# Sums of the down weights' blocks, formed in memory by adding transfers: issued one or three at a time behind named steps, with the block as the outer dimension of the scratch array

## The chip, the cores and the metric

The kernel runs on one core of a Trainium2 chip. The metric is the device time of one execution in microseconds (us), the median of several runs, lower is better. The core has TensorE (PE, matrix products), VectorE (DVE), ScalarE (ACT), GpSimd (POOL) and the SyncE queue (SP). SP, ACT and POOL issue transfers (DMAs); all of them are carried by the same 16 DMA engines. An adding transfer, whose destination becomes the sum of what it held and what arrives, is issued from POOL here.

## The reference, cut to what matters

One decoder block over 512 tokens of width 1024, all in float32:

```python
h = rms_norm(x, norm_mix_pre)
xr, gr, q, k, v, iq, ik, iw, g_a, g_b = split(h @ w_in)
y_a = (rg_lru(causal_depthwise_conv(xr)) * gelu(gr)) @ w_rnn_out
y_b = dsa_sparse_attention(rope(q), rope(k), v, iq, ik, iw) @ w_att_out   # top 128 keys of 512
merged = sigmoid(g_a) * y_a + sigmoid(g_b) * y_b
x = x + rms_norm(merged @ w_o, norm_mix_post)
h = rms_norm(x, norm_ffn_pre)
f = (silu(h @ w_ffn_gate) * (h @ w_ffn_up)) @ w_ffn_down                  # 1024 -> 2816 -> 1024
out = x + rms_norm(f, norm_ffn_post)
```

The last product, by w_ffn_down, is done with the seven-product block scheme of Strassen and Winograd. It needs sums of four 128 x 512 blocks of the weight for each of 11 pairs of row tiles; these sums are what the change is about.

## The kernel before

**Precision.** Each float32 operand is split into a high part and a low remainder (type fp32r), and a product is three matmuls: high by high, high by low, low by high (`mm3`, lines 285, 287 and 289). For most tiles of w_in the low part is made by the DMA engines: POOL loads the tile as the high part (`do_load`, line 221, 512 KB), ACT writes its negative (`do_split`, line 247), and POOL adds the tile onto that with an adding transfer (line 248). These units pass through four "ws" and four "raw" slots and are loaded a few units ahead.

**Stages.** After the input norm come the indexer, the gate and recurrence projections (lines 632 to 643), one gate, one key and two query projections (706), then eight output projections of the recurrent branch (`rnn_out(0)` to `rnn_out(7)`, line 709; weights come through SP, line 231, and DVE forms the gated result `ma[m]` at line 653). Then attention: 16 heads by 4 query tiles are 64 units (line 793). Each unit has its logits, exponentials, transposes of the probabilities (line 752) and, at the end of a head, the product with the values (762). A pair of heads ends with a split of its output into `ot` by ACT and DVE (778). Between the steps of the units, 14 remaining projections are fed in a fixed share (`fill`, line 781): six of the queries, one key tile and seven gates; queries and keys need the rotary embedding (`rope`, line 475: a shuffle on DVE, line 479, two multiplications on POOL, lines 480 and 481, and a sum on DVE, 482). Here TensorE's order is pinned to the order in the program (`state["ordered"]`). After attention come eight output projections (line 816), each with a product on DVE (819), a sum on POOL (820) and a split; then w_o, the norms and the feed-forward part.

**The sums.** For each of 11 pairs j, `u_dram[j]` (1 MB of device memory) is filled in four steps by `down_sums` (line 686): SP lays down four blocks with one transfer (692); an adding transfer of 512 KB adds a block to the first two (694); one of 256 KB adds the first to the third (696); one of 256 KB adds the third to the fourth (also 696). Each step of a pair needs the step before it. Pairs go in groups of three (GROUP = 3; the last has two), and a call of `down_sums(n)` issues step 0 of group n, step 1 of group n-1, step 2 of group n-2 and step 3 of group n-3 together: 3 to 9 transfers. There are seven calls: behind rnn_out(1) and rnn_out(5) (line 712), and in heads 2, 5, 8, 11 and 14 (line 799). In the feed-forward part `load_d` (line 1073) loads each `u_dram[j]` into two tiles of 512 KB.

**Order.** The order on each engine comes from a planner that simulates the program; every engine then runs its instructions strictly in that order. `tc.issue_after(ins)` puts what follows behind `ins` on the engine of `ins`, and does not wait for its end. A transfer that POOL issues waits on POOL until its data and its room are ready, and all that is behind it on POOL waits too.

Of the kernel before, what the change touches and what calls it, by code (L numbers as in the profile page):

```python
# [9 lines left out]
F32 = mybir.dt.float32  # L10
F32R = mybir.dt.float32r
AF = mybir.ActivationFunctionType
A = mybir.AluOpType
AX = mybir.AxisListType

P = 128
S = 512
D = 1024
KT = D // P
NT = S // P  # L20
D_FF = 2816
FT = D_FF // P
# [23 lines left out]
def hybrid_block(ctx: ExitStack, tc: tile.TileContext, x, norm_mix_pre, w_in, conv_w, conv_b, rg_w_a,  # L46
# [4 lines left out]
    V, SC, G, PE = nc.vector, nc.scalar, nc.gpsimd, nc.tensor  # L51
    ld = nc.sync.dma_start
# [5 lines left out]
    small = ctx.enter_context(tc.tile_pool(name="small", bufs=4))  # L58
# [2 lines left out]
    ps_scope = ExitStack()  # L61
    ps_mix = ps_scope.enter_context(tc.tile_pool(name="ps_mix", bufs=1, space=bass.MemoryType.PSUM))

    GROUP = 3
    dram = ctx.enter_context(tc.tile_pool(name="dram", bufs=1, space=bass.MemoryType.DRAM))

    def acc():
        return psum.tile([P, 512], F32, name="acc", tag="acc")
# [4 lines left out]
    def ps_t():  # L73
        return ps_mix.tile([P, 512], F32, name="ps_t", tag="t", bufs=2)

    def ps_o():
        return ps_mix.tile([P, 512], F32, name="ps_o", tag="o", bufs=1)

    def f(ap):
        return ap.bitcast(F32)  # L80

    after = {}

    def split(src, hi, lo, lo_engine=None):
        return SC.copy(hi, src).ins, (lo_engine or V).tensor_tensor(lo, src, f(hi), op=A.subtract).ins  # L85
# [33 lines left out]
    def heap(shape, dt=F32R, name="hp"):  # L119
        return mixp.tile(shape, dt, name=name, tag="heap", bufs=14)  # L120
# [76 lines left out]
    state = {"load": 0, "split": 0, "ordered": False}  # L197
# [64 lines left out]
    def take(u, ahead=3):  # L262
        load_ahead(u)
        while state["split"] <= min(u + ahead, state["load"] - 1):
            s = state["split"]
            if units[s][3] == "r" or s > u + 2 and units[s][3] == "s":
                break
            do_split(s)
            state["split"] += 1
        return wss.pop(u)  # L270
# [7 lines left out]
    def pe(ins):  # L278
        if state["ordered"]:
            tc.keep_in_program_order(ins)  # L280
# [11 lines left out]
    def mm3(*args, **kw):  # L292
        for _ in mm3_steps(*args, **kw):
            pass
# [77 lines left out]
    for k0 in (0, 4):  # L372
        ks = slice(k0, k0 + 4)
        for cs in (slice(0, 256), slice(256, TOKW)):
            with tc.issue_after(after["hn"]), tc.issue_after(after["sqrt"]):
                ins = split(w_tok[:, ks, cs], tokw[:, 0, ks, cs], tokw[:, 1, ks, cs], G if k0 == 0 else V)
# [69 lines left out]
    sp = mixp.tile([P, KT], F32, name="sp")  # L446
# [24 lines left out]
    ma = [map_.tile([P, S], F32, name=f"ma{m}") for m in range(KT)]  # L471
# [73 lines left out]
    def drain(n):  # L545
        for _ in range(min(n, len(background))):
            background.pop(0)()
# [101 lines left out]
    def rnn_out(m):  # L649
        ps = acc()  # L650
        mm3(ps, take(u_ya[m]), lambda k: ys[k][:, 0, :], lambda k: ys[k][:, 1, :])
        SC.activation(ma[m], ma[m], AF.Sigmoid)
        V.tensor_tensor(ma[m], ps, ma[m], op=A.mult)
# [27 lines left out]


    NJ = FT // 2
    u_dram = [dram.tile([P, 4, 512], F32, name=f"u_dram{j}") for j in range(NJ)]

    def down_sums(n):
        for step, g in enumerate(range(n, n - 4, -1)):
            for j in range(GROUP * g, min(GROUP * g + GROUP, NJ)) if g >= 0 else ():
                u = u_dram[j]
                with tc.issue_after(after["pool"]), tc.issue_after(after["sp"]):  # L690
                    if step == 0:
                        ld(u, t_dn[j])
                    elif step == 1:
                        G.dma_start(u[:, 0:2], t_dn2[j], accum_op=A.add)
                    else:
                        G.dma_start(u[:, step:step + 1], u[:, 2 * step - 4:2 * step - 3], accum_op=A.add)

    def gate_b(m):
        ps = acc()
# [9 lines left out]
    for m in range(KT):  # L709
        rnn_out(m)  # L710
        drain(4)
        if m in (1, 5):
            down_sums(m // 4)
    drain(len(background))

    pts = []
# [29 lines left out]
    def probs(u):  # L746
        h, i = divmod(u, NT)
        pt, sm = pts[h % 2], sms.pop(u)
        w = (i + 1) * P
        pp = ps_t()  # L750
        for j in range(i + 1):
            pe(PE.transpose(pp[:, j * P:(j + 1) * P], sm[:, j * P:(j + 1) * P], ident))  # L752
        src = pp[:, 0:w].rearrange("p (j c) -> p j c", c=P)
        split(src, pt[:, 0, i:4 * i + 1:3, :], pt[:, 1, i:4 * i + 1:3, :])

    def values(h):
        pt = pts[h % 2]
        ps = ps_o()
        spans = [(0, 0, 4), (1, 4, 3), (2, 8, 2), (3, 11, 2)]
        for n, (j, b, w) in enumerate(spans):  # L760
            for part in range(2):
                pe(PE.matmul(ps[:, S - w * P:S], vst[j // 2][:, j % 2, h // 4, :], pt[:, part, b:b + w, :],
                             start=(n == 0 and part == 0), stop=(n == 3 and part == 1)))
        if h % 2 == 1:
            rb, pr = state["rb"], ps_t()
            for i in range(NT):
                pe(PE.transpose(pr[:, i * P:(i + 1) * P], rb[:, i], ident))
        ob = attp.tile([HD, S], F32, name="ob", tag="ob", bufs=1)
        SC.copy(ob, ps[HD:P])
        if h % 2 == 0:  # L770
            state["o"] = attp.tile([P, S], F32, name="o", tag="o", bufs=2)
        o = state["o"]
        off = (h % 2) * HD
        V.tensor_tensor(o[off:off + HD], ps[0:HD], ob, op=A.add)
        if h % 2 == 1:
            V.tensor_tensor(o, pr, o, op=A.mult)
            ot = heap([P, 2, S], name="ot")
            split(o, ot[:, 0, :], ot[:, 1, :])
            os_.append(ot)

    def filler():
        for kind, m in fill:
            yield from {"q": queries, "k": keys, "g": gate_b}[kind](m)
# [9 lines left out]
    for u in range(n_units):  # L793
        if u + AHEAD < n_units:
            logits(u + AHEAD)
        probs(u)
        if u % NT == LAG and u >= NT:
            values(u // NT - 1)
            if u // NT % 3 == 2:
                down_sums(2 + u // NT // 3)  # L800
        while done < START + (u + 1) * (n_fill - START) // n_units:
            next(fills, None)
            done += 1
# [5 lines left out]
    gb = []  # L809
    for m in range(KT):  # L810
        t = tmpp.tile([P, S], F32, name="gb", tag="t0")
# [4 lines left out]
    for m in range(KT):  # L816
        ps = acc()
        mm3(ps, take(u_yb[m]), lambda k: os_[k][:, 0, :], lambda k: os_[k][:, 1, :])
        V.tensor_tensor(gb[m], ps, gb[m], op=A.mult)
        G.tensor_tensor(gb[m], gb[m], ma[m], op=A.add)  # L820
        t = heap([P, 2, S], name="mg")
        split(gb[m], t[:, 0, :], t[:, 1, :])
        mg.append(t)
# [67 lines left out]
    for t in range(NT):  # L891
# [16 lines left out]
        r = neg2_rstd(ss[:, 0:1], 1, ss[:, 1:2])  # L908
# [161 lines left out]
    w_dn = w_ffn_down.rearrange("(j e p) c -> e p j c", e=2, p=P)  # L1070
    raw_d, ws_d, as_d = {}, {}, {}

    def load_d(j):
        raw_d[j] = []
        for c in range(2):
            t = raw_tile(c, [P, 2, 512])
            ld(t, u_dram[j][:, 2 * c:2 * c + 2, :])
            raw_d[j].append(t)

    def prep_d(j):  # L1080
# [23 lines left out]
    NJ = FT // 2  # L1104
# [178 lines left out]
```

## Time and profile before

| | us |
|---|---|
| median of three runs (907.73 to 910.62) | 908.67 |
| the profiled execution | 908.55 |
| its span, first to last instruction | 906.8 |
| TensorE busy in it | 850.8 |
| DVE busy | 678.1 |
| ACT busy | 524.1 |
| POOL busy | 259.5 |

A profiled execution records each instruction with its engine, start and duration, and for idle time of an engine the instruction or transfer that ended it (the releaser). TensorE is busy for most of the span, so the places to look at are those where it is not. The granted clock of TensorE is shown per stretch as a share: 1.00 is its higher level (2.4 GHz), 0.5 its lower one (1.2 GHz). The share of the DMA engines counts the time of packets, which can overlap, so it can be above 1. "Landing" is the time from a transfer's issue to the arrival of its last data.

### The profile page before, as it was taken

What the parts mean: (1) busy time and instruction counts of PE and PEld (TensorE: products, weight loads), DVE (VectorE), ACT (ScalarE), POOL (GpSimd) and SP (SyncE); (2) the same over time, 40 slices, a digit from 0 to 9 for tenths busy, and PEclk for the clock granted to TensorE, in tenths of its full rate; (3) what the DMA queues carried; (4) which work ended last, traced back from release to release, by engine and by line L of the source; (5) the groups of instructions that cost most, each with busy time, mean ns of one, the idle gap of its engine ahead of it and who ended that gap; (6) DMA issues with size and microseconds to landing.
All of it is one profiled execution on the core that took longest, in us unless ns stands there. A gap on an engine that the chain in (4) does not pass through costs nothing.

```text
span 906.8 us, 13184 instructions
## 1 busy us (share of the span) xinstructions
PE 850.8 (94%) x4745; PEld 735.5 (81%) x4745; DVE 678.1 (75%) x1235; ACT 524.1 (58%) x902; POOL 259.5 (29%) x276
## 2 busy tenths in 40 slices
PE   8999999999897989498999998899999999999996
PEld 5787888877686778487878887799999999988885
DVE  6686989976851487357756647988888788799996
ACT  5355457978321778376754435666566656566581
POOL 3262234552502444253002200233333333110000
PEclk9999999999899899799999999999999999999999
DMA  8488888759599797998354563667787878847623
GB/s 291 102 173 186 163 161 175 162 125 259 163 319 195 164 168 195 176 209 165 116 161 152 186 199 116 162 162 172 189 180 178 181 181 189 215 161 236 203 93 139
DMA packets 75316, 161.46 MB, mean 178 GB/s; under 512 B 9858, under 2 KB 33474, under 8 KB 75075
## 3 DMA queue, kind: packets, MB, share of 16 engines
q0 software_dynamic: 23184, 73.41, 42.3%
q1 hardware_dynamic: 50912, 85.11, 29.2%
q10 hardware_dynamic: 1154, 2.10, 0.6%
q8 instruction: 37, 0.61, 0.3%
q14 instruction: 29, 0.23, 0.1%
HBM read 154.31 MB, written 29.36 MB: 203 GB/s over the span
## 4 chain that ended last, share of the span: by engine, by line
PE 53%; DVE 14%; DMA 12%; issue 9%; ACT 6%; POOL 4%; SPq 1%; DVEq 0%; ACTq 0%; POOLq 0%
PE acc L285 6%; PE acc L287 6%; PE acc L289 6%; DMA ws<-in_t_ff_dram 5%; PE bank L1012 5%; PE bank L1010 4%; PE bank L1011 4%; PE bank L1102 2%; PE bank L1100 2%; PE bank L1101 2%; DVE xc L585 2%; PE acc L1010 2%; PE acc L1011 1%; PE acc L1012 1%; DMA ws<-in_t_in_dram 1%
## 5 line engine op out<-in xcount | busy, mean ns | idle before, releaser
L289 PE MATMUL acc<-hT,ws 128*128 128x512 f32 x248 | 99.8, 403 | 7.2 <-DMA ws<-in_t_in_dram 7.2
L85 DVE TENSOR_TENSOR ws<-raw,ws 128x1024 fp32r<-128x1024 f32 (+1 forms) x66 | 85.7, 1308 | 26.9 <-ACT ws L85 26.9
L285 PE MATMUL acc<-hT,ws 128*128 128x512 f32 x248 | 99.9, 403 | 1.4 <-ACT xpad L581 1.4
L85 ACT CAST ws<-raw 128x1024 fp32r<-128x1024 f32 (+1 forms) x66 | 67.2, 1032 | 58.7 <-PE acc L289 20.2
L287 PE MATMUL acc<-hT,ws 128*128 128x512 f32 x248 | 100.0, 403 | 0.0
L1004 POOL DMA_DIRECT2D ws<-in_t_ff_dram x40 | 35.2, 888 | 155.6 <-PE bank L1012 90.1
L85 ACT CAST ws<-sums 128x1024 fp32r<-128x1024 f32 x40 | 40.3, 1048 | 52.3 <-DVE sums L994 42.3
L289 PEld LDWEIGHTS acc<-hT,ws 128*128 128x128 f32 x248 | 47.5, 191 | 17.7 <-DMA ws<-in_t_in_dram 7.7
L1010 PE MATMUL bank<-T,ws 128*128 128x256 f32 x200 | 57.2, 286 | 2.5 <-ACT ws L85 2.5
L1012 PE MATMUL bank<-T,ws 128*128 128x256 f32 x200 | 58.7, 294 | 0.9 <-DMA ws<-in_t_ff_dram 0.6
L285 PEld LDWEIGHTS acc<-hT,ws 128*128 128x128 f32 x248 | 47.5, 192 | 12.0 <-ACT xpad L581 1.8
L1011 PE MATMUL bank<-T,ws 128*128 128x256 f32 x200 | 56.9, 285 | 0.0
L1011 PE MATMUL bank<-B,ws 128*128 128x256 f32 x200 | 56.3, 282 | 0.0
L1010 PE MATMUL bank<-B,ws 128*128 128x256 f32 x200 | 56.1, 281 | 0.0
L287 PEld LDWEIGHTS acc<-hT,ws 128*128 128x128 f32 x248 | 47.6, 192 | 10.1
L1012 PE MATMUL bank<-B,ws 128*128 128x256 f32 x200 | 55.7, 279 | 0.0
L85 DVE TENSOR_TENSOR ws<-sums,ws 128x1024 fp32r<-128x1024 f32 x40 | 47.8, 1232 | 8.7 <-ACT ws L85 8.7
L736 DVE CUSTOM_DVE_ANT_0 sm<-ps_s,mask 128x256 f32<-128x256 f32 (+1 forms) x64 | 33.1, 521 | 26.1 <-PE ps_s L731 26.0
L285 PE MATMUL acc<-hT,raw 128*128 128x512 f32 x120 | 48.0, 400 | 1.0 <-ACT gl L573 1.0
L287 PE MATMUL acc<-hT,raw 128*128 128x512 f32 x120 | 48.1, 401 | 0.0
L289 PE MATMUL acc<-hT,raw 128*128 128x512 f32 x120 | 47.7, 398 | 0.0
L752 PE MATMUL ps_t<-ident,sm 128*128 128x128 f32 x160 | 28.6, 277 | 18.7 <-DVE pt L85 18.7
(366 smaller groups left out, 2754.6 us busy)
## 6 DMA issues: line engine op xcount, KB each, us to landing
ws<-in_t_in_dram POOLq DMA_DIRECT2D x58, 512.0 KB, 6.1
raw<-in_t_ff_dram SPq DMA_DIRECT2D x40, 512.0 KB, 3.7
raw<-in_t_in_dram POOLq DMA_DIRECT2D x30, 512.0 KB, 6.5
raw<-u_dram SPq DMA_DIRECT2D x22, 512.0 KB, 5.5
ws<-in_t_ff_dram POOLq DMA_DIRECT2D x20, 512.0 KB, 5.6
raw<-in_w_ffn_down_dram SPq DMA_DIRECT2D x15, 512.0 KB, 3.7
u_dram<-in_t_dn_dram POOLq DMA_DIRECT2D x11, 512.0 KB, 13.3
u_dram<-u_dram POOLq DMA_DIRECT2D x22, 256.0 KB, 13.2
```

The source lines that it names most:

```text
L85: return SC.copy(hi, src).ins, (lo_engine or V).tensor_tensor(lo, src, f(hi), op=A.subtract).ins
L285: pe(PE.matmul(ps, ws[0][:, k, :], hi(k), start=(n == 0), stop=False))
L287: pe(PE.matmul(ps, ws[0][:, k, :], lo(k), start=False, stop=False))
L289: pe(PE.matmul(ps, ws[1][:, k, :], hi(k), start=False, stop=(n == len(order) - 1)))
L585: V.scalar_tensor_tensor(xc, xp[:, j:j + S], col(j, m), xc, op0=A.mult, op1=A.add)
L736: V.tensor_tensor_reduce(sm[:, 0:n], ps[:, 0:n], masks[i], 1.0, -LOW, A.add, A.min, mn)
L752: pe(PE.transpose(pp[:, j * P:(j + 1) * P], sm[:, j * P:(j + 1) * P], ident))
L1004: G.dma_start(dst[:, 1], t_ff[n, m].rearrange("p (k c) -> p k c", c=P)[:, k], accum_op=A.add)
L1010: PE.matmul(ps, a[:, 0, k, :], b[:, 0, k, :], start=(k == 0), stop=False)
L1011: PE.matmul(ps, a[:, 0, k, :], b[:, 1, k, :], start=False, stop=False)
L1012: PE.matmul(ps, a[:, 1, k, :], b[:, 0, k, :], start=False, stop=(k == 3))
L1100: PE.matmul(ps, a[:, 0, ts], b[:, 0], start=first, stop=False)
```

## The change

The grouped calls go, and with them GROUP. The adding transfers stand in a list `adds`, for each j: step 1 of pair j, step 2 of pair j-1, step 3 of pair j-2 (an entry without a pair is empty). A call of `down_sums(paced, n)` first makes POOL copy one column of `paced` into a small tile `pace`, then issues the next n entries of the list behind that copy. It is called behind each of the eight `rnn_out(m)` with one column of `ma[m]` and n = 1, behind the split of each of the eight head pairs with one column of `ot` and n = 3, and behind the sum of each of the eight attention output projections with one column of `gb[m]` and n = 1. The list has 39 entries, 33 of them real. With every third entry SP lays down the blocks of one more pair (`lay_down`), two pairs ahead of their first adding transfer; pairs 0, 1 and 2 are laid down behind rnn_out(0).

`u_dram[j]` changes its layout: the four blocks stand one after the other, each as 64 rows of 4 KB, where before each of 128 rows held its four pieces of 2 KB. The host lays out the inputs accordingly. The adding transfers are cut into pieces (descriptors) of 4 KB at most. `load_d` reads through a view that restores the 128 rows, of which each now consists of two pieces of 2 KB per tile.

```diff
-    u_dram = [dram.tile([P, 4, 512], F32, name=f"u_dram{j}") for j in range(NJ)]
-
-    def down_sums(n):
-        for step, g in enumerate(range(n, n - 4, -1)):
-            for j in range(GROUP * g, min(GROUP * g + GROUP, NJ)) if g >= 0 else ():
-                u = u_dram[j]
-                with tc.issue_after(after["pool"]), tc.issue_after(after["sp"]):
-                    if step == 0:
-                        ld(u, t_dn[j])
-                    elif step == 1:
-                        G.dma_start(u[:, 0:2], t_dn2[j], accum_op=A.add)
-                    else:
-                        G.dma_start(u[:, step:step + 1], u[:, 2 * step - 4:2 * step - 3], accum_op=A.add)
+    u_dram = [dram.tile([4, P // 2, 2 * S], F32, name=f"u_dram{j}") for j in range(NJ)]
+    adds = []
+    for j in range(NJ + 2):
+        adds.append(lambda j=j: (u_dram[j][0:2], t_dn2[j]) if j < NJ else None)
+        adds.append(lambda j=j: (u_dram[j - 1][2], u_dram[j - 1][0]) if 0 <= j - 1 < NJ else None)
+        adds.append(lambda j=j: (u_dram[j - 2][3], u_dram[j - 2][2]) if 0 <= j - 2 else None)
+    state["add"] = 0
+
+    def lay_down(j):
+        if j < NJ:
+            with tc.issue_after(after["sp"]):
+                ld(u_dram[j], t_dn[j])
+
+    def down_sums(paced, n=1):
+        pace = small.tile([P, 1], F32, name="pace")
+        ins = G.tensor_copy(pace, paced).ins
+        for _ in range(n):
+            i = state["add"]
+            if i >= len(adds):
+                return
+            state["add"] += 1
+            if i % 3 == 0:
+                lay_down(i // 3 + 2)
+            step = adds[i]()
+            if step is not None:
+                with tc.issue_after(ins):
+                    G.dma_start(step[0], step[1], accum_op=A.add, max_dma_last_dim=4096)
...
         rnn_out(m)
         drain(4)
-        if m in (1, 5):
-            down_sums(m // 4)
+        if m == 0:
+            lay_down(0)
+            lay_down(1)
+        down_sums(ma[m][:, 0:1])
...
             split(o, ot[:, 0, :], ot[:, 1, :])
             os_.append(ot)
+            down_sums(f(ot[:, 1, 0:1]), 3)
...
             values(u // NT - 1)
-            if u // NT % 3 == 2:
-                down_sums(2 + u // NT // 3)
...
         G.tensor_tensor(gb[m], gb[m], ma[m], op=A.add)
+        down_sums(gb[m][:, 0:1])
...
+    def u_view(j):
+        return u_dram[j].rearrange("b q (r c) -> b (q r) c", r=2).rearrange("b p c -> p b c")
+
...
-            ld(t, u_dram[j][:, 2 * c:2 * c + 2, :])
+            ld(t, u_view(j)[:, 2 * c:2 * c + 2, :])
```

## Rows read from the trace of the kernel before

**Rows 1.** TensorE's idle time: start us, us, instruction, and in brackets idle before, releaser

```profile
296.82 0.79 PE L289 MATMUL acc<-hT,ws 128*128 128x512 f32 x1 [7.24 <-DMA ws<-in_t_in_dram]
...
333.43 0.66 PE L752 MATMUL ps_t<-ident,sm 128*128 128x128 f32 x2 [3.26 <-DVE pt L85]
...
380.86 0.69 PE L752 MATMUL ps_t<-ident,sm 128*128 128x128 f32 x2 [11.76 <-DVE pt L85]
...
410.85 0.44 PE L752 MATMUL ps_t<-ident,sm 128*128 128x128 f32 x2 [3.26 <-DVE pt L85]
```

**Rows 2.** Timeline of DVE in attention, the same columns

```profile
327.72 2.91 DVE L488 TENSOR_TENSOR qst<-rp_x,qst 64x512 fp32r<-64x512 f32 x1
...
379.51 0.69 DVE L482 TENSOR_TENSOR rp_x<-rp_x,rp_s 128x512 f32<-128x512 f32 x1 [13.38 <-POOL rp_s L481]
...
409.50 0.69 DVE L482 TENSOR_TENSOR rp_x<-rp_x,rp_s 128x512 f32<-128x512 f32 x1 [4.64 <-POOL rp_s L481]
```

**Rows 3.** Timeline of POOL in attention, the same columns

```profile
327.21 1.61 POOL L480 TENSOR_TENSOR rp_x<-rp_x,rope_c 128x512 f32<-128x512 f32 x1
...
350.66 2.58 POOL L694 DMA_DIRECT2D u_dram<-in_t_dn_dram  x3
352.30 4.32 POOL L696 DMA_DIRECT2D u_dram<-u_dram  x4
366.47 0.82 POOL L696 DMA_DIRECT2D u_dram<-u_dram  x1 [9.85 <-issue]
...
376.98 1.28 POOL L480 TENSOR_TENSOR rp_x<-rp_x,rope_c 128x512 f32<-128x512 f32 x1
...
401.38 1.75 POOL L696 DMA_DIRECT2D u_dram<-u_dram  x2 [0.77 <-issue]
```

**Rows 4.** Timeline of POOL just before attention, the same columns

```profile
236.89 0.31 POOL L719 MEMSET pt<- 128x256 f32 x1
...
275.52 0.90 POOL L248 DMA_DIRECT2D raw<-in_t_in_dram  x1 [11.12 <-ACT raw L247]
...
276.76 2.78 POOL L694 DMA_DIRECT2D u_dram<-in_t_dn_dram  x3
```

**Rows 5.** Timeline of SP just before attention, the same columns

```profile
250.93 3.74 SPq L692 DMA_DIRECT2D u_dram<-in_t_dn_dram  x6
```

**Rows 6.** Transfers issued at 235 to 262 us: queue, count, KB each, median landing

```profile
raw<-in_t_in_dram POOLq DMA_DIRECT2D x1, 512.0 KB, 17.5
```

**Rows 7.** Transfers issued at 276 to 283 us, the same columns

```profile
raw<-in_t_in_dram POOLq DMA_DIRECT2D x1, 512.0 KB, 5.5
```

**Rows 8.** Chain that ended last, 225 to 410 us: start us, us, what

```profile
283.81 12.96 DMA ws<-in_t_in_dram
...
297.62 0.43 PE acc L285
...
302.52 0.23 PE acc L285
...
381.55 2.35 PE ps_o L762 x8
...
390.82 1.29 PE ps_o L762 x8
```

**Rows 9.** Stretches: length, busy PE, PEld, DVE, ACT, POOL; PEclk, DMA share, GB/s

```profile
390.00:405.00 15.00, 15.00 (x88) 13.04 (x87) 9.99 (x31) 10.38 (x27) 6.85 (x9) 1.00 1.08 190
...
750.00:800.00 50.00, 49.82 (x389) 48.20 (x388) 40.49 (x62) 29.45 (x39) 13.14 (x11) 1.00 0.79 203
```

**Rows 10.** Profile page, DMA queues: packets, MB, share of 16 engines over the span

```profile
q0 software_dynamic: 23184, 73.41, 42.3%
q1 hardware_dynamic: 50912, 85.11, 29.2%
```

**Rows 11.** Profile page, loads of the last product: count, KB each, median landing

```profile
raw<-u_dram SPq DMA_DIRECT2D x22, 512.0 KB, 5.5
...
raw<-in_w_ffn_down_dram SPq DMA_DIRECT2D x15, 512.0 KB, 3.7
```

More of the change, by code (lines that the diff above doesn't have):

```diff
@@ L62, in hybrid_block @@
     ps_mix = ps_scope.enter_context(tc.tile_pool(name="ps_mix", bufs=1, space=bass.MemoryType.PSUM))
-    GROUP = 3
     dram = ctx.enter_context(tc.tile_pool(name="dram", bufs=1, space=bass.MemoryType.DRAM))
@@ L1269 @@
     blocks = {f"{e + 1}{c + 1}": dn[:, :, e, c] for e in range(2) for c in range(2)}
-    named.append(("t_dn", _np.stack([blocks[n] for n in ("11", "22", "22", "21")], axis=2)))
-    named.append(("t_dn2", _np.stack([blocks["12"], blocks["12"]], axis=2)))
+    named.append(("t_dn", _np.stack([blocks[n] for n in ("11", "22", "22", "21")], axis=1).reshape(FT // 2, 4, P // 2, 2 * S)))
+    named.append(("t_dn2", _np.stack([blocks["12"], blocks["12"]], axis=1).reshape(FT // 2, 2, P // 2, 2 * S)))
     for name, a in named:
```

## The prediction, written before the change was run

> **What bounds the kernel now.** I read the releasers of TensorE's idle time first. Nearly all of it between the projections and the end of attention lies in four gaps [rows 1]: 7.24, 3.26, 11.76 and 3.26 us. Elsewhere in attention TensorE is full: 15.00 of 15 us in a stretch [rows 9] where the share of the DMA engines is 1.08. So a busy DMA is not yet a stall; what matters is who is held up, and where. I followed each gap back.
>
> The **long gap** ends at 380.86 on a probability split by DVE. DVE had stood 13.38 us for the rotary embedding on POOL [rows 2]. POOL had issued three adding transfers (line 694) and four more (line 696) in a row; the eighth came after a pause of 9.85 us [rows 3]. That pause ends on "issue", nothing the profile can name; in this group POOL stops once seven adding transfers are outstanding, so I read it as lack of room for their descriptors. The embedding that stood behind them began at 376.98, 24.7 us after the group of four [rows 3]. The **gap at 410.85** is the next group: POOL issues line 696 with pauses [rows 3], and DVE waits 4.64 us for the embedding [rows 2].
>
> The **first gap** ends at 296.82 with a low part of a projection weight. Its adding transfer was issued at 283.81 and took 12.96 us [rows 8], behind three adds to the sums issued from 276.76 on [rows 4]. It was also issued late: POOL had stood 11.12 us for a weight in a raw slot [rows 4], whose plain load took 17.5 us [rows 6] where the next raw transfer, an adding one, took 5.5 [rows 7]. That load ran beside six transfers of 1 MB that SP put out together from 250.93 on [rows 5]. The **gap at 333.43** has another cause: a split on DVE of 2.91 us [rows 2], no sum is involved.
>
> After each of the gaps TensorE runs for a while at the lower of its two clock levels (1.2 of 2.4 GHz): 0.43 us per matmul until about 302.3, then 0.23 [rows 8].
>
> **What the change removes.** Step by step, against the profiled execution's 908.6 us (the median of 908.67 is the same for this purpose):
>
> 1. The long gap, 11.76 us [rows 1], and the slow matmuls behind it: 2.35 - 1.29 = 1.1 us on the one product of a head [rows 8]. Three adds behind each head pair take the place of groups of up to nine transfers, so seven are never outstanding, and what POOL puts ahead of an embedding is three issues. Gain 12.9.
> 2. The gap at 410.85: 3.26 [rows 1], and 1 us of low clock, an estimate from step 1. Gain 4.3.
> 3. The first gap: 7.24 [rows 1] and, from 296.82 to 302.3, some 13 matmuls at 0.43 in place of 0.23, 2.6 us [rows 8]. Gain 9.8. Two things must hold. SP's burst of six becomes three (pairs 4, 5 and 6, all placed behind the last output weight; pair 3 goes earlier, 0 to 2 as before). At 264.8 us for 85.11 MB on SP's queue, 3.1 us per MB [rows 10], the three missing ones are 9.8 us, so the load of 17.5 should land 8 to 10 us sooner, and the chain behind it starts sooner. And the three adds of 512 KB ahead of the low part become at most one of 512 and one of 256 KB. By 383.6 us for 73.41 MB, 5.2 us per MB on POOL's queue [rows 10], the three were 8.2 us and what replaces them is at most 4.1. TensorE needs the data at 289.6 (296.82 - 7.24). Without the earlier start it would come at 283.81 + 12.96 - 4.1 = 292.7, 3.1 us late; with it, in time. I take the whole gap as gone; the bounds are 0 and 9.8.
>
> The gap at 333.43 I leave in place; it may go or come anywhere, as two engines' orders shift: 0 to 4.3 us to the good.
>
> **What it adds and moves.** The 33 adds and their 11.5 MB stay, about 60 us of the DMA engines by 5.2 us per MB, now spread from the first output projection to the eighth output projection of attention. The last of them fall behind attention, past its four gaps, and long before the feed-forward part reads the sums. Each add needs one issued at least a head pair, or some projections, earlier, so POOL should not stand for data.
>
> The 24 pace copies are new. Nothing like them is in the trace; the nearest row is a memset of 0.31 us on POOL [rows 4], far larger than one column. POOL has the room, so I take nothing, at most 24 x 0.31 = 7.4 us. The Trainium skill, page SBUF — State Buffer, section SBUF: two separate sides, speaks against them: the port pair shared by DVE and GpSimd is held by one of them for the whole instruction, and a DVE operation with two SBUF inputs and a GpSimd operation that reads SBUF block each other. The trace agrees in kind: the split of 2.91 us began at 327.72, during a multiplication of the embedding that POOL began at 327.21 [rows 2, 3]; by the page all 24 would at worst add the 7.4 us to DVE's path, and the sum would be 893 and not 886.
>
> The real cost of a pace copy is its wait. POOL stands until DVE has written `ma`, `ot` or `gb`, and behind it in POOL's order are weight loads, low parts, embeddings; for the embeddings DVE waits, and for DVE the transposes of TensorE. In the price of such a collision the trace helps: DVE late by 2.2 us (2.91 less the usual 0.69 of that split, the same 0.69 as the sum of an embedding) cost TensorE 3.26 us [rows 1, 2], with the clock 4.4. Three issues of some 0.8 us ahead of an embedding are of the same size. There are seven embeddings in attention; the planner puts a pace copy where it expects its data, so most should miss. Between 0 and 7 x 4.4 = 30.8 I take one, 4.4 us.
>
> The 4 KB pieces: the 256 KB adds have half as many descriptors, and this frees room on POOL's side; per byte I expect nothing. The reverse, 2 KB pieces in the loads of `u_dram` by SP, has a row: the weight loads of the last product, cut alike, land in 3.7 us, those of `u_dram` with 4 KB in 5.5 [rows 11]. They are issued two pairs ahead, and TensorE is busy 49.82 of 50 us there [rows 9]. So 0. If that cover were gone, 1 or 2 us at the first pair.
>
> **The sum**: 908.6 - 12.9 - 4.3 - 9.8 + 4.4 = 886.0 us.
>
> **The rivals.**
> A, *the first gap stays, or the transfers bind.* For: laying down still comes in threes, and POOL's order may put several adds behind the late load, as before. With gaps shorter, a head pair needs 1 MB of adds and 1.75 MB of projection weights at 5.2 us and 1 MB of laying down at 3.1, together 17.4 us; two products of heads stand 9.3 us apart, 8.2 without the slow start [rows 8], so a pair has 16.4. Against: full work at a share of 1.08 [rows 9]. Then step 3 is lost: 895.8.
>
> B, *it doesn't spread.* The adds are paced by POOL's own order; if POOL is still held by late weights, they bunch as before, and a pause moves instead of going. Against: no more than three are put behind one pair. Then 903 to 909, no change, 907.
>
> C, *slower: the pace copy holds the embedding.* If in POOL's order the pace copy stands ahead of an embedding whose input is ready, the embedding waits for the pair's last split on DVE and then for three issues. At 4.4 us for each of seven embeddings the loss is 30.8 against a gain of 27.0: 912. It decides only from the seventh on, or if each costs more than 3.9 us, as one like the wait of 13.38 would [rows 2]. Against: the planner orders by its own simulated times, and ropes and pair ends are not in step (seven against eight).
>
> **How the numbers follow.** My forecast 0.55; A 0.22; B 0.08; C 0.10; and 0.05 that the 333 us gap goes too and no collision comes, 908.6 - 27.0 - 4.3 = 877. Everything up to A counts as faster by over 0.3%, which is 2.7 us here and about what a measurement of this kernel can tell from no change: 0.82, with half of B's lower end 0.84. B gives the rest of no change and some partial results, 0.06; C 0.10. The range from 875 to 903 leaves out C and most of B, under 2 in 10, and takes in the bounds of the pace copies' cost (893) and of step 3 (895.8), with one or two more collisions.
>
> **What would show it.** Right: no idle of TensorE over 5 us between 285 and 470; no pause of POOL before an add that ends on "issue"; DVE's waits for POOL's embedding under 3 us; SP's burst at 251 of three; the raw load near 8 us; adds landing in 5 to 9 us. Step 3 is wrong if a wait of TensorE for `ws` stays near 289. C shows as waits of POOL at the pace line for DVE with embeddings right behind. The prediction fails if the new order of some engine brings a stall in a stage that none of these rows touches, since the planner redoes the whole order.

## The result and the profile after

| | before | changed |
|---|---|---|
| median, same chip, us | 909.64 (907.73 to 912.58) | 884.55 (882.38 to 885.09) |
| the profiled execution | 908.55 | 885.09 |
| its span | 906.8 | 883.3 |

The ratio is 0.9717, with a 95% interval from 0.9684 to 0.975: 25 us faster. On a second chip (change_again, below) it was 0.9744 [0.9709 to 0.9779].

From the profile page of the changed kernel: busy time of the engines, the DMA queue of POOL (packets, MB, share of 16 engines), then DMA issues (count, KB each, median us to landing). The queue's row answers to [rows 10], the loads of `u_dram` to [rows 11].

```profile
PE 847.3 (96%) x4745; PEld 733.3 (83%) x4745; DVE 676.1 (77%) x1235; ACT 522.5 (59%) x902; POOL 268.1 (30%) x300
q0 software_dynamic: 21776, 73.41, 42.4%
raw<-u_dram SPq DMA_DIRECT2D x22, 512.0 KB, 4.5
u_dram<-in_t_dn_dram POOLq DMA_DIRECT2D x11, 512.0 KB, 8.4
u_dram<-u_dram POOLq DMA_DIRECT2D x22, 256.0 KB, 7.3
```

The adding transfers land in 8.4 and 7.3 us. On the page of before it was 13.3 and 13.2:

```profile
u_dram<-in_t_dn_dram POOLq DMA_DIRECT2D x11, 512.0 KB, 13.3
u_dram<-u_dram POOLq DMA_DIRECT2D x22, 256.0 KB, 13.2
```

TensorE's gaps between the projections and the attention output come next (timeline: start us, us, instruction, in brackets the idle time before it and what ended it). They answer to [rows 1].

```profile
295.55 0.47 PE L767 MATMUL ps_t<-ident,sm 128*128 128x128 f32 x1 [2.06 <-ACT sm L752]
...
323.57 0.44 PE L767 MATMUL ps_t<-ident,sm 128*128 128x128 f32 x2 [0.97 <-DVE pt L84]
...
443.26 0.79 PE L284 MATMUL acc<-ot,ws 128*128 128x512 f32 x1 [2.86 <-ACT ot L84]
```

Four gaps of 3.26 to 11.76 us have become two of 2.06 and 0.97, and there is one new gap of 2.86 us, at the attention output. What makes the 2.06 us at 295.55 was not followed. The POOL rows that answer to [rows 3] show how a set of adds now stands ahead of an embedding:

```profile
373.43 0.18 POOL L698 COPY pace<-ot 128x1 f32<-128x1 f32 x1 [0.50 <-DVE ot L84]
373.67 0.80 POOL L709 DMA_DIRECT2D u_dram<-u_dram  x1
374.24 1.10 POOL L709 DMA_DIRECT2D u_dram<-in_t_dn_dram  x1
374.78 1.40 POOL L709 DMA_DIRECT2D u_dram<-u_dram  x1
375.31 2.18 POOL L479 TENSOR_TENSOR rp_x<-rp_x,rope_c 128x512 f32<-128x512 f32 x1
```

From the copy to the embedding it is 1.9 us, where the group of four of before held the embedding for 24.7 us [rows 3]. In the views of waits (us in total, times, longest; DVE's from 280 to 470 us, POOL's from 240 to 520) DVE's wait for the embedding, 13.38 us at its worst in [rows 2], is almost nothing. What waits now is the pace copy behind the head pairs, for 50.8 us in all, and POOL has that time:

```profile
DVE rp_x L481 <- POOL rp_s L480: 0.7, 2, 0.4
POOL pace L698 <- DVE ot L84: 50.8, 7, 16.2
```

**Where the time went.** The same three products of TensorE, before (first fence) and changed (second fence): the first and the last product with the values, and a product with w_o.

```profile
313.33 1.53 PE L762 MATMUL ps_o<-pt,vst 128*128 128x512 f32 x8
...
461.06 1.73 PE L762 MATMUL ps_o<-pt,vst 128*128 128x512 f32 x8
...
529.60 0.40 PE L896 MATMUL acc<-wo,mg 128*128 128x512 f32 x1
```

```profile
305.62 1.53 PE L777 MATMUL ps_o<-pt,vst 128*128 128x512 f32 x8
...
433.44 1.71 PE L777 MATMUL ps_o<-pt,vst 128*128 128x512 f32 x8
...
506.86 0.40 PE L911 MATMUL acc<-wo,mg 128*128 128x512 f32 x1
```

Up to the first values product 7.7 us are gained (313.33 - 305.62); up to the last 27.6, so attention itself gives 19.9; up to w_o 22.7, so the attention output gives 4.9 back. The end comes 23.5 us earlier (906.8 - 883.3), 0.8 more. These are single executions. The profile of the same kernel in change_again has its first values product 6.1 us earlier than before, attention again 19.9 shorter, and the attention output gives 2.4 back: the 19.9 repeat, the parts on either side move by 2 us or so. The gap at the attention output is there too (2.82 us), but the granted clock from 435 to 500 us is 1.00 in place of 0.95.

The 4.9 us have a place. ACT's rows, before (first fence) and changed (second fence), show the first output weight of attention coming later relative to the last values product:

```profile
464.85 1.05 ACT L85 CAST ws<-raw 128x1024 fp32r<-128x1024 f32 x1 [1.45 <-DMA raw<-in_w_att_out_dram]
```

```profile
439.71 1.05 ACT L84 CAST ws<-raw 128x1024 fp32r<-128x1024 f32 x1 [3.93 <-DMA raw<-in_w_att_out_dram]
...
442.60 0.60 ACT L84 CAST ot<-o 128x512 fp32r<-128x512 f32 x1
```

ACT starts that cast 3.8 us behind the start of the last values product before and 6.3 behind it in the changed kernel; the split of `ot` stands behind the cast on ACT, TensorE waits 2.86 us for it, and then runs at the low clock level for a while (granted clock 0.83 from 430 to 450).

### The profile page after: what moved, and what is told of

Same layout as the page of the kernel before. It is cut to its first block, busy times and chain, and to the rows that moved or that the text cites. A ratio compares the mean times of both kernels' runs of the same rounds, so it can differ in the third digit from the quotient of the medians.

```text
span 883.3 us, 13217 instructions
## 1 busy us (share of the span) xinstructions
PE 847.3 (96%) x4745; PEld 733.3 (83%) x4745; DVE 676.1 (77%) x1235; ACT 522.5 (59%) x902; POOL 268.1 (30%) x300
## 3 DMA queue, kind: packets, MB, share of 16 engines
q0 software_dynamic: 21776, 73.41, 42.4%
## 4 chain that ended last, share of the span: by engine, by line
PE 62%; DVE 13%; DMA 9%; ACT 7%; issue 6%; POOL 1%; SPq 1%; DVEq 0%; ACTq 0%; POOLq 0%
PE acc L284 7%; PE acc L286 7%; PE acc L288 7%; PE bank L1027 5%; PE bank L1026 4%; PE bank L1025 4%; DMA ws<-in_t_ff_dram 3%; PE bank L1118 3%; PE bank L1119 3%; PE bank L1120 3%; PE ps_o L777 2%; PE ps_t L767 2%; DVE xc L584 2%; PE acc L1026 2%; PE acc L1025 2%
## 5 line engine op out<-in xcount | busy, mean ns | idle before, releaser
L284 PE MATMUL acc<-hT,ws 128*128 128x512 f32 x248 | 98.8, 398 | 1.4 <-ACT xpad L580 1.4
L286 PE MATMUL acc<-hT,ws 128*128 128x512 f32 x248 | 99.0, 399 | 0.0
L288 PE MATMUL acc<-hT,ws 128*128 128x512 f32 x248 | 98.7, 398 | 0.0
L1027 PE MATMUL bank<-T,ws 128*128 128x256 f32 x200 | 57.7, 289 | 2.2 <-DMA ws<-in_t_ff_dram 1.9
L1025 PE MATMUL bank<-T,ws 128*128 128x256 f32 x200 | 56.5, 283 | 0.2 <-ACT ws L84 0.2
L284 PEld LDWEIGHTS acc<-hT,ws 128*128 128x128 f32 x248 | 46.7, 188 | 11.9 <-ACT xpad L580 1.9
L1026 PE MATMUL bank<-T,ws 128*128 128x256 f32 x200 | 56.4, 282 | 0.0
L286 PEld LDWEIGHTS acc<-hT,ws 128*128 128x128 f32 x248 | 46.7, 188 | 10.0
L288 PEld LDWEIGHTS acc<-hT,ws 128*128 128x128 f32 x248 | 46.7, 188 | 9.8
L1010 POOL TENSOR_TENSOR sums<-raw 128x512 f32<-128x512 f32 x20 | 33.1, 1655 | 36.3 <-PE bank L1027 12.1
```

What stands on the lines that cost most here:

```text
L284: pe(PE.matmul(ps, ws[0][:, k, :], hi(k), start=(n == 0), stop=False))
L286: pe(PE.matmul(ps, ws[0][:, k, :], lo(k), start=False, stop=False))
L288: pe(PE.matmul(ps, ws[1][:, k, :], hi(k), start=False, stop=(n == len(order) - 1)))
L1010: G.tensor_tensor(s3, a11, a21, op=A.subtract)
L1025: PE.matmul(ps, a[:, 0, k, :], b[:, 0, k, :], start=(k == 0), stop=False)
L1026: PE.matmul(ps, a[:, 0, k, :], b[:, 1, k, :], start=False, stop=False)
```

## The experiments

The theory that the experiments test: the change gains because no group of adds holds POOL's queue, (W) the wait for data in the pace copy is what spreads them, the pause in the long gap is a lack of room for descriptors, and (S) the first gap went with SP's burst of six. Rivals: the 4 KB layout alone does it; (Q) the three adds ahead of the low part made the first gap; (C) what is left to gain are the adds that still run beside the first loads of the attention output. Ratios are to the kernel before on the same chip.

**1. layout_only.** The kernel before, with the new layout and the 4 KB pieces, but its own groups.

```diff
-    u_dram = [dram.tile([P, 4, 512], F32, name=f"u_dram{j}") for j in range(NJ)]
+    u_dram = [dram.tile([4, P // 2, 2 * S], F32, name=f"u_dram{j}") for j in range(NJ)]
...
-                        G.dma_start(u[:, step:step + 1], u[:, 2 * step - 4:2 * step - 3], accum_op=A.add)
+                        G.dma_start(u[step], u[2 * step - 4], accum_op=A.add, max_dma_last_dim=4096)
```

> The kernel before with the new layout and 4 KB pieces alone; the sums stay in their groups of three pairs. Theory G (the grouping itself holds POOL): the group of nine still stands ahead of an embedding, the long gap stays at 8 to 12 us, total 900 to 909. Rival R (room: POOL stops because descriptors of seven adding transfers fill it, and halving those of the 256 KB adds makes room): no pause of POOL before an add that ends on issue, the gaps of 11.76 and 3.26 us go, total 889 to 895.

893.6 us, ratio 0.9855 [0.9812 to 0.9897], so half of the gain comes without any pacing. The group that made the long gap, on POOL, and the end of that gap on TensorE:

```profile
348.99 2.61 POOL L694 DMA_DIRECT2D u_dram<-in_t_dn_dram  x3
350.60 5.04 POOL L696 DMA_DIRECT2D u_dram<-u_dram  x5
361.91 0.78 POOL L696 DMA_DIRECT2D u_dram<-u_dram  x1 [6.27 <-DMA u_dram<-in_t_dn_dram]
```

```profile
372.26 0.69 PE L752 MATMUL ps_t<-ident,sm 128*128 128x128 f32 x2 [4.78 <-DVE pt L85]
```

POOL issues eight adds instead of seven before it stops, the stop is 6.27 us instead of 9.85 [rows 3], and the gap is 4.78 instead of 11.76 [rows 1]. Behind it no gap over 1.1 us is left in attention, where before had 3.26 at 410.85; the first gap (5.88 us) and the one near 330 (3.25) stay. Attention takes 138.4 us from the first to the last values product, 147.7 before.

**2. room_3072.** The kernel before with half as much again of memory for the descriptors of POOL's transfers: the reading "lack of room" by itself.

```diff
-    nc = _bacc.Bacc("TRN2", target_bir_lowering=False, num_devices=1, dynamic_dma_scratch_size=2048)
+    nc = _bacc.Bacc("TRN2", target_bir_lowering=False, num_devices=1, dynamic_dma_scratch_size=3072)
```

> The kernel before with half as much again of memory for POOL's descriptors (3072 in place of 2048 bytes per partition), nothing else. If the pause of 9.85 us is lack of room, POOL issues ten or more adding transfers without one: R expects the pause and the gaps of 11.76 and 3.26 us to go, total 889 to 895. G expects the group to be issued without a pause, but weight loads to stand behind it in the queue, so that a wait for weights takes the place of part of the gap: 895 to 905. If it is not room, nothing changes: 907 to 911.

906.07 us, ratio 0.9983 [0.9959 to 1.0007]: no change clear of noise.

```profile
350.30 2.58 POOL L694 DMA_DIRECT2D u_dram<-in_t_dn_dram  x3
351.92 5.17 POOL L696 DMA_DIRECT2D u_dram<-u_dram  x5
365.63 0.81 POOL L696 DMA_DIRECT2D u_dram<-u_dram  x1 [8.55 <-DMA u_dram<-in_t_dn_dram]
370.96 0.90 POOL L248 DMA_DIRECT2D ws<-in_t_in_dram  x1 [4.51 <-DMA u_dram<-in_t_dn_dram]
```

```profile
378.23 0.69 PE L752 MATMUL ps_t<-ident,sm 128*128 128x128 f32 x2 [9.43 <-DVE pt L85]
```

The room gave one more add, eight for seven, as half the pieces did in layout_only. Then POOL stops for 8.55 us all the same, now until one of the adds lands. If seven filled the room, half as much again would have held ten, and POOL stopped at eight; so I read room as a limit with a second one right behind it. How soon the first adds land decides the length of the stop, and that the layout shortens.

**3. paced_2k and paced_2k_again.** The changed kernel with the layout and the 2 KB pieces of before: the pacing alone, on two chips.

```diff
-        adds.append(lambda j=j: (u_dram[j - 1][2], u_dram[j - 1][0]) if 0 <= j - 1 < NJ else None)
+        adds.append(lambda j=j: (u_dram[j - 1][:, 2:3], u_dram[j - 1][:, 0:1]) if 0 <= j - 1 < NJ else None)
...
-                    G.dma_start(step[0], step[1], accum_op=A.add, max_dma_last_dim=4096)
+                    G.dma_start(step[0], step[1], accum_op=A.add)
```

> The changed kernel with the old layout: 2 KB pieces for the 256 KB adds, 4 KB pieces in the loads of the last product. Theory G: never more than three adds and two or three weight transfers are outstanding, so room is not reached and nothing is lost: 882 to 888, within 0.5% of the changed kernel. Rival R: with twice the descriptors for 22 of 33 adds the pauses come back in part: 890 to 898.

> The changed kernel with the old layout, a second time, beside the changed one. The first time it stood at 0.981 of the kernel before, the changed one in another session at 0.972. If the layout adds something to the pacing (an eighth transfer in room, sums that land sooner), it is again 3 to 7 us above the changed kernel. If the pacing alone does it, the two agree within 2 us.

889.31 us, ratio 0.9813 [0.9766 to 0.986], and 890.05, 0.9813 [0.9784 to 0.9841]. Beside the second ran **change_again**, the changed kernel unaltered:

> The changed kernel as it is, on the same chip as the three beside it, so that they can be compared with it: ratio to the kernel before 0.968 to 0.976.

882.88 us, 0.9744 [0.9709 to 0.9779]. Pacing alone gains 17 us, and the layout adds 7 on top of it. Both together give less than the sum of each alone (17 and 13), for both shorten the same long gap. The page of paced_2k_again shows the queue of POOL and the adds:

```profile
q0 software_dynamic: 23184, 73.41, 43.6%
u_dram<-in_t_dn_dram POOLq DMA_DIRECT2D x11, 512.0 KB, 9.7
u_dram<-u_dram POOLq DMA_DIRECT2D x22, 256.0 KB, 8.5
```

By share times span POOL's queue takes 388.3 us of the 16 engines (43.6% of 890.7), in the changed kernel 374.5 (42.4% of 883.3), for the same 73.41 MB with 1408 packets less. The adds land 1.3 and 1.2 us later. On TensorE the loss is not in attention: from the first to the last values product it takes 127.6 and 127.8 us in the two profiles with 2 KB pieces, 127.8 in both profiles of the changed kernel. The part that shows is the attention output, from the last values product to w_o: 75.3 and 76.1 us against 73.4 and 71.0. There TensorE is busy 58.81 of the 65 us from 435 to 500 in paced_2k_again, 62.14 in the changed kernel, and paced_2k_again has a gap of 2.89 us at 468.59 that the others have not.

**4. no_pace_copy.** The changed kernel without the copy that waits for data: the same calls, the adds only placed in POOL's order by the planner.

```diff
-        pace = small.tile([P, 1], F32, name="pace")
-        ins = G.tensor_copy(pace, paced).ins
...
-                with tc.issue_after(ins):
+                with tc.issue_after(after["pool"]):
```

> The changed kernel without the 24 pace copies: the adds stand at the same places in the program but wait for nothing but their own data and the last weight load traced before them on POOL. Theory W (the data wait spreads them): the planner puts them as early as their data allows, several stand ahead of a load or an embedding, pauses of POOL and gaps of 3 us and more come back, 888 to 900. Rival P (the place in the program is enough): 880 to 887, and if the copies cost something, 1 to 3 us below the changed kernel.

892.63 us, ratio 0.9847 [0.9817 to 0.9876], 10 us slower than change_again beside it. POOL's rows, and the gaps of TensorE:

```profile
395.90 0.78 POOL L707 DMA_DIRECT2D u_dram<-u_dram  x1 [10.44 <-DMA u_dram<-u_dram]
396.41 1.18 POOL L247 DMA_DIRECT2D ws<-in_t_in_dram  x1
```

```profile
405.08 0.47 PE L765 MATMUL ps_t<-ident,sm 128*128 128x128 f32 x1 [7.14 <-DVE pt L84]
...
422.15 0.49 PE L765 MATMUL ps_t<-ident,sm 128*128 128x128 f32 x2 [5.03 <-DVE pt L84]
```

The adds run ahead and bunch; one stands 10.44 us on POOL until an earlier add lands, and the low part of a weight stands behind it. W holds: the calls alone do not spread the adds, the wait does.

**5. lay_down_six.** The changed kernel, but SP lays the blocks down in its old bursts of three and six (theory S).

```diff
-            if i % 3 == 0:
-                lay_down(i // 3 + 2)
+            for j in {9: (6, 7, 8), 15: (9, 10)}.get(i, ()):
+                lay_down(j)
...
-        if m == 0:
-            lay_down(0)
-            lay_down(1)
+        for j in {0: (0, 1, 2), 5: (3, 4, 5)}.get(m, ()):
+            lay_down(j)
```

> The changed kernel with SP's laying down in groups again (three, then six at once behind the last output weight, then two); POOL's adds are paced as in the change. Theory S (the six transfers of 1 MB made the first gap, through a weight load of 17.5 us): the raw load lands in 16 to 18 us again, the first gap returns by 3 to 8 us, total 888 to 894. Rival Q (the three adds ahead of the low part made it): the load is slow again but no gap comes, total 883 to 886.

881.98 us, ratio 0.9727 [0.967 to 0.9783]: the time of the changed kernel. SP's burst, the landing of the raw load (issues from 235 to 262 us) and the gap on TensorE:

```profile
251.72 4.05 SPq L694 DMA_DIRECT2D u_dram<-in_t_dn_dram  x6
```

```profile
raw<-in_t_in_dram POOLq DMA_DIRECT2D x1, 512.0 KB, 20.6
```

```profile
291.16 0.50 PE L288 MATMUL acc<-hT,ws 128*128 128x512 f32 x1 [1.89 <-DMA ws<-in_t_in_dram]
```

The burst is back and the raw load takes 20.6 us, even longer than the 17.5 of [rows 6]; yet TensorE waits only 1.89 us. S falls.

**6. first_adds_late.** The kernel before, with the three adds that stood ahead of the low part moved into attention (theory Q).

```diff
-    def down_sums(n):
+    def down_sums(n, lo=0, hi=4):
         for step, g in enumerate(range(n, n - 4, -1)):
+            if not lo <= step < hi:
+                continue
...
-            down_sums(m // 4)
+            down_sums(m // 4, 0, 1)
...
             if u // NT % 3 == 2:
+                if u // NT == 2:
+                    down_sums(1, 1)
                 down_sums(2 + u // NT // 3)
```

> The kernel before, with one edit: the three 512 KB adds that stood behind the sixth output projection are issued in attention instead, at the third head pair, ahead of the group that stands there already. Theory Q: the first gap (7.24 us before, on a low part of a projection weight) was made by the three adds that lay ahead of that low part in POOL's queue; then the low part lands in under 8 us after its issue, the gap on ws is under 3 us, and TensorE's first values product starts 5 to 8 us sooner. Rival R: the chain is late because POOL stood behind the raw load of 17.5 us, whatever lies in the queue; then the gap stays at 5 to 8 us. Under both the group in attention grows from seven adds to ten, so the long gap stays or grows (10 to 20 us), and the total time is 900 to 912.

905.86 us, ratio 0.9998 [0.9979 to 1.0016]. POOL's stop, the landing of the low part issued at 283.89 us (issues from 283 to 284), and TensorE:

```profile
275.41 0.90 POOL L248 DMA_DIRECT2D raw<-in_t_in_dram  x1 [12.25 <-ACT raw L247]
```

```profile
ws<-in_t_in_dram POOLq DMA_DIRECT2D x1, 512.0 KB, 5.8
```

```profile
289.78 0.50 PE L289 MATMUL acc<-hT,ws 128*128 128x512 f32 x1 [1.44 <-DMA ws<-in_t_in_dram]
305.24 1.53 PE L764 MATMUL ps_o<-pt,vst 128*128 128x512 f32 x8
...
335.57 0.45 PE L754 MATMUL ps_t<-ident,sm 128*128 128x128 f32 x1 [5.47 <-DVE pt L85]
...
376.64 0.69 PE L754 MATMUL ps_t<-ident,sm 128*128 128x128 f32 x2 [11.63 <-DVE pt L85]
```

POOL still stands for the late raw load (12.25 us, [rows 4] 11.12), but the low part issued at the same time lands in 5.8 us instead of 12.96 [rows 8], the gap is 1.44 and the first values product starts at 305.24, where the changed kernel has 305.62. Q holds: the three adds made the first gap. The long gap stays at 11.63 us, the 333 us gap is larger (5.47 for 3.26), and at the end nothing is left that the timed runs can see. In the profile attention takes 3.2 us longer than before (150.9 against 147.7), which is part of the 8.1 gained ahead of it; where the rest goes is not shown. A gap removed ahead of a stall that the adds set is not yet time.

**7. four_per_pair.** The changed kernel with four adds behind each of the first six pairs and none behind the last two, so that none runs beside the first loads of the attention output (theory C). This moves the six adds of the last two pairs forward.

```diff
-            down_sums(f(ot[:, 1, 0:1]), 3)
+            if len(os_) <= 6:
+                down_sums(f(ot[:, 1, 0:1]), 4)
```

> The changed kernel with four entries of the list behind each of the first six head pairs and none behind the last two, so that no add is in flight while the first weights of the attention output are loaded. Theory C (adds of the seventh pair slow that load, ScalarE waits 3.9 us for it, and TensorE stands 2.9 us at 443.26 and goes on at half clock): the gap shrinks below 1 us, 878 to 882. Rival (the load is late by SP's own order of gate loads and stores): the gap stays, 883 to 887. If four adds per pair are too many, POOL pauses and gaps come back in attention: 886 to 892.

878.35 us, ratio 0.9687 [0.966 to 0.9715], 4.5 us faster than change_again beside it (0.9744 [0.9709 to 0.9779]; the intervals just overlap), and the fastest that computes everything. First the loads of the output weight issued in the stretch around the end of attention, in the changed kernel (425 to 437 us) and here (415 to 437), then ACT's row here:

```profile
raw<-in_w_att_out_dram SPq DMA_DIRECT2D x2, 512.0 KB, 6.5
```

```profile
raw<-in_w_att_out_dram SPq DMA_DIRECT2D x2, 512.0 KB, 4.8
```

```profile
436.68 1.05 ACT L84 CAST ws<-raw 128x1024 fp32r<-128x1024 f32 x1 [1.67 <-DMA raw<-in_w_att_out_dram]
```

SP's loads land in 4.8 us without adds beside them and in 6.5 with them, ACT waits 1.67 us instead of 3.93, and TensorE 0.6 instead of 2.86. C holds: the attention output takes 68.7 us again, as in the kernel before (68.5), in no_pace_copy (68.5) and in no_adds (68.7), none of which issues an add there before the first weight is split; with adds there it is 71.0 to 76.1. Attention itself is 1.8 us longer with four adds behind a pair (129.6 for 127.8), and the profile is 2.6 to 4.2 us ahead of the two of the changed kernel at the first values product already, where the two programs do not differ; so how much of the 4.5 us is C's is not shown exactly. The Trainium skill, page DMA: Bandwidth & Descriptors, section Queues, rings and completion order, says that each DMA engine takes turns between the queues that have work, a packet at a time; the rows agree, with a load of SP's queue slower by 1.7 us beside POOL's adds.

**8. no_adds.** The changed kernel without its 33 adding transfers (so the feed-forward part reads partial sums); copies and laying down stay.

```diff
-            if step is not None:
+            if False:
```

> The changed kernel with its 33 adding transfers left out; the pace copies and the laying down stay, so the feed-forward part reads partial sums. It tells what the adds still cost after the change. If the 5.0 us given back at the attention output and the small gaps are the adds' (theory C), the time is 5 to 10 us below the changed kernel, 873 to 878, and TensorE has no gap over 1 us between 430 and 450. If the rest is the planner's order and the pace copies, the time is within 2 us of the changed kernel, 881 to 885.

876.19 us, ratio 0.9684 [0.9646 to 0.9723], the ratio of four_per_pair. TensorE has no gap over 0.8 us between 322 and 534. From its page:

```profile
q0 software_dynamic: 18432, 61.87, 35.8%
```

That is 314.9 us of the engines (35.8% of 879.7), so the adds take 59.6 us in the changed kernel (374.5) and 73.4 in paced_2k_again (388.3): the small pieces cost a fourth more. Single profiles differ: five of paced kernels with the 4 KB layout give 372 to 378 us for the queue, the two with 2 KB pieces 387 and 388. By the ratios (0.9717 and 0.9744 for the change) the adds still cost the changed kernel 3 to 5 us, and four behind each pair hide even those. None of it is in attention, which takes 127.8 us without adds and with them.

**9. room_1024_after.** The changed kernel with half the memory for descriptors.

```diff
-    nc = _bacc.Bacc("TRN2", target_bir_lowering=False, num_devices=1, dynamic_dma_scratch_size=2048)
+    nc = _bacc.Bacc("TRN2", target_bir_lowering=False, num_devices=1, dynamic_dma_scratch_size=1024)
```

> The changed kernel with half the memory for descriptors of POOL's transfers (1024 in place of 2048). If the pacing keeps so few transfers outstanding that room never counts, the time stays within 0.3% of the changed kernel, 880 to 886, and POOL has no wait over 3 us ahead of an add. If the paced kernel still uses the room of seven, POOL stops ahead of adds or weight loads for 5 us and more, and the time rises to 890 to 905.

881.67 us, ratio 0.9731 [0.9701 to 0.9761], no different from the change, and 5.5 us above no_adds on the same chip; POOL's longest wait ahead of an add is 0.4 us. Paced, the adds never need more than half of the room.

## Why the prediction was right, and where its steps were not

The forecast was 886.0 and the result 884.55, but the steps carry different errors that partly cancel: 17.2 us forecast for steps 1 and 2, 9.8 for step 3 and 4.4 for the collision became 19.9, 7.7 and 4.9 in the profiles. And 7 of the 25 us are the layout's, which the text put at 0; the pacing alone measured 17. So the mechanism was right, and the close sum is in part luck.

**Steps 1 and 2, the gaps in attention: right in place and size, the reason only in part.** Both gaps are gone, and no embedding is held. With the 333 us gap, which the text left in place and gave as a bonus of up to 4.3, it makes 21.5 us; 19.9 were measured. But the 9.85 us pause was not only "lack of room for their descriptors". With more room POOL issues one add more and stops again (experiment 2). What the pacing takes away is the whole burst of seven or eight adds ahead of an embedding, the last of them held until earlier ones land, whatever the limit is.

**The 333 us gap.** It shrank to 0.97 us with the new order, by chance as the text held possible. The slow kind of operation that had made it is still there, on a split of `ot`; the split of probabilities behind it on DVE is the one that TensorE awaits at 323.57. DVE's rows of the changed kernel (first fence) and POOL's of the same time (second fence):

```profile
320.02 2.90 DVE L84 TENSOR_TENSOR ot<-o,ot 128x512 fp32r<-128x512 f32 x1
322.84 0.68 DVE L84 TENSOR_TENSOR pt<-ps_t,pt 128x512 fp32r<-128x512 f32 x1
```

```profile
319.49 1.62 POOL L479 TENSOR_TENSOR rp_x<-rp_x,rope_c 128x512 f32<-128x512 f32 x1
320.74 1.62 POOL L480 TENSOR_TENSOR rp_s<-rp_s,rope_s 128x512 f32<-128x512 f32 x1
322.98 0.18 POOL L698 COPY pace<-ot 128x1 f32<-128x1 f32 x1 [0.62 <-DVE ot L84]
```

A split of 2.90 us beside POOL's multiplications, as in [rows 2, 3]; the pace copy, at 0.18 us, slows nothing: the next split takes its 0.68. The rule that the prediction weighed, in the Trainium skill's page SBUF — State Buffer, section SBUF: two separate sides, has the first row on its side. For the copies its price did not come. The eight behind head pairs take 1.5 us in all; all 24 take 11.7 us of POOL, for those close behind its other work are longer, which is more than the bound of 7.4, but the excess lies outside attention.

**Step 3, the first gap: 7.7 us, not 9.8, and of its two reasons one fell.** "With it, in time" was to come from the smaller burst of SP. The burst is smaller (three transfers at 250.63), but the raw load still takes 11.7 us, not about 8, and with the burst of six put back the time is the same (experiment 5). The other reason, adds ahead of the low part, explains the gain at this place: experiment 6 takes only them away and starts attention as early as the changed kernel. What of it reaches the end is not shown, for alone it brought no time. The 2.1 us short of 9.8 are the size of the new gap of 2.06 at 295.55. The error was a sum of two causes where one alone ends last: POOL's 11 us for a raw slot [rows 4] was idle time that TensorE's work in hand covered (in experiment 6 POOL stands 12.25 us, and the gap is 1.44).

**The collision: 4.4 us forecast, 4.9 and 2.4 in the two profiles of the changed kernel, but another one.** The text expected a pace copy or three issues to hold an embedding. None did: DVE's waits for embeddings are 0.7 us in all in attention, and rival C did not show although the copies wait 50.8 us. What came is that adds of the seventh pair run beside SP's load of the first output weight. The text looked for the cost in POOL's queue, and the price lay in the DMA engines, in the stage that starts on a fresh load. That the first profile matched the size is chance.

**"Per byte I expect nothing" was wrong.** The 4 KB layout takes 13.8 us off the DMA engines' work (388.3 - 374.5; 9 to 16 between other profiles of the paced kernels) and is worth 13 us in the old grouping and 7 in the paced one. The prediction could have bounded it: nothing in the trace of before showed a 256 KB add of 4 KB pieces, so "nothing" had no row behind it. The pieces of 2 KB in the loads of `u_dram` cost nothing, as expected (4.5 us, 5.5 before [rows 11]).

**The rivals.** A (the first gap stays) and B (it does not spread) did not occur; experiment 4 shows that B's mechanism is real as soon as the wait for data is left out.

**Open.** Why half the pieces save as much as they do is not settled, nor where all of the 7 us lie: the attention output shows 2 to 5 of them. Nor is it known what the second limit of POOL is. It seems to count weight transfers too: in the next group of layout_only POOL stops after seven adds, for 0.77 us, until a weight load lands. More room than 3072 was not tried.

## What to carry to other kernels

Spread background transfers by a tiny operation that waits for data of the step they belong to; order alone did not spread them here, and a copy costs 0.18 to 1.07 us on an engine with time to spare. Keep them out of the stretch where a stage begins on a freshly loaded weight: moving six adds away from it measured the same ratio as leaving all 33 out (0.9687 and 0.9684, on two chips). When a wait in a profile ends on "issue", test what the limit is before you count on lifting it.

## What the runs showed of the hardware

In the group of nine, with one weight load issued just ahead, POOL stopped after seven adds with 2 KB pieces and 2048 of descriptor memory, and after eight both with half the pieces and with 3072; in the last two runs the ninth waits for a landing. For the same bytes in the paced kernels, 256 KB adds between two places of device memory in 64 pieces of 4 KB took a fifth less of the DMA engines' time, over all adds, than in 128 of 2 KB (59.6 against 73.4 us in one profile each; 57 to 63 and 72 to 73 over all). And six 1 MB copies on SP's queue stretched one 512 KB load on POOL's to 20.6 us at no cost to the kernel.
